# An encoder trunk in fp32: the gates' rows turned to one chunk per partition, the heads' rows repeated over the partitions by DMA, values projected first and the output gate last

## The chip, the core and the metric

The kernel runs on one core of a Trainium2 chip. The metric is the device time of one execution in microseconds (us). A core has a matrix engine (TensorE: PE in the profile, its weight loads PEld), a vector engine (VectorE: DVE), a scalar engine (ScalarE: ACT), a further elementwise engine (GpSimd: POOL) and a queue engine that here only issues transfers (SyncE: SP). Each engine works through its own instructions in order; semaphores hold an instruction until those of other engines, or transfers, are done. On chip, data lie in SBUF (128 partitions) and in PSUM, which the matrix engine writes. DRAM is the large memory off chip.

## What is computed

Two layers over a sequence of 1024 positions with width 1024. Each layer has an mLSTM group (4 heads of 128), a dilated attention group (8 heads of 64), an output projection and a feed-forward part of 4096. The change lies in the mLSTM group alone:

```
h = rms_norm(x, norm1_g); proj = h @ w_in
mq, mk, mv, mo, mi, mf, aq, ak, av = split(proj)
mq, mk = silu(depthwise_conv5([mq, mk]))
gi = mi + gate_i_b                       # 2 directions x 4 heads, a row of 1024 each
gf = log_sigmoid(mf + gate_f_b)
h_fwd = mlstm_chunkwise(q, k, v, gi[0], gf[0])
h_bwd = flip(mlstm_chunkwise(flip(q), flip(k), flip(v), flip(gi[1]), flip(gf[1])))
hm = headwise_rms(h_fwd + h_bwd) * head_norm_g
y_m = hm * sigmoid(mo)
```

Within a chunk the gates are needed as b = cumsum(lf), as a running maximum of li - b, and as a maximum m that is carried from chunk to chunk. Of these come a factor exp(li - b - max) for each pair of positions in a chunk, a factor for q against the state that comes in, and a decay of that state.

## The kernel before

Activations lie transposed: features on partitions, the 1024 positions in the free dimension. A projection (`proj`, 128 output features) is 48 matmuls 128x512: 8 blocks of input features, 2 halves of the positions (t = 0 and 1), and 3 products of split operands (`mm3`, lines 90 to 92). Its weights come in two loads of 256 KB on SP's queue (`wload`, line 73); each is split into a high part by ACT (line 80) and a low part by POOL (line 82), with three buffers for each of `wr`, `wh` and `wl`. The results stand in PSUM banks `pj` (three) and DVE copies them out, times the norm's factor r (`evac_r`, line 173).

`gates` makes one projection whose 128 rows repeat 16 gate rows (8 input, 8 forget), so every partition carries some gate row over all 1024 positions. All of the gates' arithmetic (lines 216 to 274) runs on 128x1024 tiles `g`: biases, log-sigmoid, two cumulative sums and two running maxima (`TENSOR_TENSOR_SCAN`, restarted at each chunk by a tile of resets), the chunk recurrence on tiles of 8 columns, and three exponentials. It leaves MT and inter (a row for each direction and head, repeated in each quarter of the partitions) and `nat`, in which three rows' worth of values are turned to one position per partition by 24 small transposes on PE (line 279) and three copies (line 280).

Then, for each head: `m_proj` projects the output gate (so, line 173), q and k (each with a 5-tap convolution, line 303, on DVE, and a sigmoid) and last v (zv), which PE transposes (line 327). `m_head` repeats the head's row of MT and of inter over all partitions with a stream shuffle on DVE, for both directions (E, line 340, and qi, line 347), adds the mask on POOL (341), subtracts on DVE (342) and takes the exponential on ACT (344). PE then turns k (358) and multiplies k with q (364), DVE multiplies E with that (366), and a chain over the 8 chunks in both directions follows, in which PE (378, 380, 389) and DVE (394) take turns for some 16 us. The matmuls of the next head's projections lie between those of the chain. `m_tail` normalises and gates the head's result; it was called between the next head's `m_proj` and its `m_head`.

The order on each engine is set by a scheduler that goes by the order of the code, by priorities (line 80 to 82 and 173 have a raised one) and by its own estimate of when each operand is ready. Tiles with a tag share a fixed number of buffers; a tile's first writer waits for the last reader of the tile that had the buffer. E, qi, kn and H of a head (and before them the gates' tiles) share the seven buffers of tag G.

## Time and profile before

| | us |
|---|---|
| median of 3 runs (2648.67 to 2659.3) | 2658.03 |
| the profiled execution, own time | 2652.92 |
| its span in the trace | 2651.2 |
| layer 0, norm's end and gates to the first chain over chunks | 24.9 to 110.3 |
| layer 0, to the second, third and fourth chain | 167.7, 233.3, 297.4 |
| layer 1, the same points | 1336.0, 1417.8, 1476.6, 1541.2, 1605.2 |

The profile is of one execution. Times within it count from the start of the span. A row of the timeline shows when an instruction began, its duration, engine, line, what it writes and reads, and in brackets how long the engine had been idle before it and what ended that. [...] Matmuls are pipelined, so two that follow one another overlap in the rows; what counts is the distance of their starts.

### The profile page before, as it was taken

Reading aid. Unit: us, or ns where it says so; the run is one execution under the profiler, and the core shown is the slowest. Engines: PE = TensorE matmul, PEld = TensorE weight load, DVE = VectorE, ACT = ScalarE, POOL = GpSimd, SP = SyncE. Lnnn points to the kernel's source line nnn. Section 1 sums busy time; section 2 is a strip of 40 time slices with the busy share of each in tenths; the row PEclk is TensorE's granted clock in tenths of the full one; section 3 lists DMA queues with packets and bytes.
Section 4 is the critical chain, followed back from the end, with each engine's and each line's share of the span. In section 5 each row is a group of like instructions: output and inputs, shape, how many; then the busy total and the mean of one; then the engine's idle time right before and its main releaser. Section 6 shows DMA issues by size and latency. Waiting matters only on the chain. (4 is left out here: it accounts for less than half of the span.)

```text
span 2651.2 us, 36031 instructions
## 1 busy us (share of the span) xinstructions
PE 2476.5 (93%) x13508; PEld 1958.3 (74%) x13508; DVE 1994.6 (75%) x2440; ACT 1269.2 (48%) x2092; POOL 1395.1 (53%) x1135
## 2 busy tenths in 40 slices
PE   7889989998999999999989898999988999999997
PEld 5777766665778888787767777666666788888876
DVE  7877656688887786968788776666788867869687
ACT  5433344464654545445534444444546445354554
POOL 5333332235677677767643333222256766677765
PEclk9999999998999999999999999999989999999998
DMA  4000110036455455555320011001355555456553
GB/s 134 29 27 30 36 35 21 25 108 148 96 111 112 103 108 112 110 109 111 85 75 29 32 33 35 24 25 38 107 132 96 112 113 107 107 104 115 112 104 84
DMA packets 113326, 214.07 MB, mean 81 GB/s; under 512 B 13424, under 2 KB 15616, under 8 KB 113152
## 3 DMA queue, kind: packets, MB, share of 16 engines
q0 software_dynamic: 46912, 93.06, 21.3%
q1 hardware_dynamic: 66240, 118.71, 14.6%
q8 instruction: 107, 1.75, 0.3%
q14 instruction: 67, 0.55, 0.1%
HBM read 203.33 MB, written 8.39 MB: 80 GB/s over the span
## 5 line engine op out<-in xcount | busy, mean ns | idle before, releaser
L82 POOL TENSOR_TENSOR wl<-w,wh 128x512 fp32r<-128x512 f32 x484 | 768.8, 1610 | 311.5 <-ACT wh L80 311.1
L812 PE MATMUL ph<-b,wh 128*128 128x512 f32 x2240 | 695.0, 392 | 13.6 <-DVE x L818 7.0
L812 PEld LDWEIGHTS ph<-b,wh 128*128 128x128 f32 x2240 | 422.6, 189 | 103.4 <-ACT wh L80 8.3
L80 ACT CAST wh<-w 128x512 fp32r<-128x512 f32 x484 | 298.2, 618 | 412.6 <-PE ph L812 119.3
L812 PE MATMUL ph<-b,wl 128*128 128x512 f32 x1120 | 441.5, 394 | 8.6 <-POOL wl L82 8.0
L82 POOL TENSOR_TENSOR wl<-wr,wh 128x512 fp32r<-128x512 f32 x132 | 198.6, 1506 | 470.6 <-ACT wh L80 385.4
L812 PE MATMUL pj<-b,wh 128*128 128x512 f32 x1224 | 383.6, 395 | 9.8 <-ACT wh L80 8.0
L90 PE MATMUL pj<-hh,wh 128*128 128x512 f32 x896 | 368.9, 412 | 18.0 <-DVE z L173 10.8
L92 PE MATMUL pj<-hh,wl 128*128 128x512 f32 x896 | 358.3, 400 | 1.2 <-POOL wl L82 0.6
L91 PE MATMUL pj<-hl,wh 128*128 128x512 f32 x896 | 358.5, 400 | 0.0
L761 DVE TENSOR_TENSOR b<-T,b 128x1024 fp32r<-128x1024 f32 x148 | 253.0, 1714 | 114.3 <-ACT b L760 110.9
L812 PEld LDWEIGHTS pj<-b,wh 128*128 128x128 f32 x1224 | 233.0, 191 | 61.2 <-ACT wh L80 9.8
L812 PEld LDWEIGHTS ph<-b,wl 128*128 128x128 f32 x1120 | 211.2, 189 | 64.8 <-POOL wl L82 21.5
L812 PE MATMUL pj<-b,wl 128*128 128x512 f32 x612 | 242.1, 396 | 8.9 <-POOL wl L82 8.9
L90 PEld LDWEIGHTS pj<-hh,wh 128*128 128x128 f32 x896 | 171.3, 191 | 68.8 <-issue 15.0
L92 PEld LDWEIGHTS pj<-hh,wl 128*128 128x128 f32 x896 | 171.1, 191 | 36.4 <-POOL wl L82 1.0
L91 PEld LDWEIGHTS pj<-hl,wh 128*128 128x128 f32 x896 | 171.4, 191 | 30.2 <-issue 0.5
L760 ACT CAST b<-T 128x1024 fp32r<-128x1024 f32 x148 | 155.6, 1051 | 58.0 <-DVE T L776 19.7
L600 ACT ACTIVATE sm<-sm,nm 128x512 f32<-128x512 f32 x128 | 91.6, 717 | 131.5 <-DVE nm L598 131.5
L788 POOL DMA_DIRECT2D w<-w_down x128 | 115.7, 933 | 73.6 <-DMA w<-w_down 23.2
L788 POOL DMA_DIRECT2D w<-w_up x128 | 113.0, 907 | 60.1 <-POOL wl L82 26.6
L812 PEld LDWEIGHTS pj<-b,wl 128*128 128x128 f32 x612 | 116.6, 191 | 36.7 <-POOL wl L82 12.4
(257 smaller groups left out, 4342.1 us busy)
## 6 DMA issues: line engine op xcount, KB each, us to landing
w<-w_up SPq DMA_DIRECT2D x128, 256.0 KB, 2.7
w<-w_up POOLq DMA_DIRECT2D x128, 256.0 KB, 4.2
w<-w_down SPq DMA_DIRECT2D x128, 256.0 KB, 2.7
w<-w_down POOLq DMA_DIRECT2D x128, 256.0 KB, 4.2
wr<-w_in SPq DMA_DIRECT2D x116, 256.0 KB, 2.7
w<-w_out SPq DMA_DIRECT2D x32, 256.0 KB, 5.2
w<-w_out POOLq DMA_DIRECT2D x32, 256.0 KB, 6.0
wr<-w_out SPq DMA_DIRECT2D x16, 256.0 KB, 2.8
```

The costliest lines, as they stand in the source:

```text
L80: nc.scalar.copy(wh, raw)
L82: nc.gpsimd.tensor_tensor(out=wl, in0=raw, in1=wh.bitcast(F32), op=ALU.subtract)
L90: nc.tensor.matmul(ps, wh[:, j, :], xh[:, sl], start=start, stop=False)
L91: nc.tensor.matmul(ps, wh[:, j, :], xl[:, sl], start=False, stop=False)
L92: nc.tensor.matmul(ps, wl[:, j, :], xh[:, sl], start=False, stop=stop)
L600: nc.scalar.activation(sm, sm, AF.Exp, scale=-1.0, bias=nm, accum_out=l)
L760: nc.scalar.copy(hi, src)
L761: nc.vector.tensor_tensor(out=lo, in0=src, in1=hi.bitcast(F32), op=ALU.subtract)
L788: self.nc.gpsimd.dma_start(w, src, accum_op=ALU.add)
L812: nc.tensor.matmul(out, a[:, k, :], b, start=new and k + i == 0, stop=k + i == 5, skip_group_check=not new)
```

## The change

`gates` now gives its work out in three steps (`next(gates, None)`, after the convolutions of q and of k in the first head's `m_proj`). The gate projection's rows, zt, are cut into their 8 chunks, and 8 small transfers on SP's queue bring them to one chunk and one gate row per partition (z: 16 rows x 8 chunks = 128 partitions, 128 positions each). All tiles of the gates' arithmetic are 128x128 from then on, in slices of two tiles X. What is carried between chunks lies across partitions now: a matmul with a 0/1 matrix `sel` (line 253, tile pa) collects it. MT and inter go to DRAM in 8 transfers (gd, line 269). The 24 small transposes become 3 of 128x128 (line 276) and one copy.

In `m_head` the shuffles of lines 340 and 347 are gone: E and qi are loaded by transfers that read the head's row of 4 KB in DRAM once for each partition (lines 339 and 346, 512 KB each, 4 for a head). `m_proj` projects v first (and turns it after q), then q, k, and the output gate last. `m_tail` of the head before is called inside `m_head`, behind the products of k and q.

```diff
     def gates(self, L, hs, acc, pl, order):
...
-        ws = [self.wload(self.a["w_in"][L, 1, :, 4 * i:4 * i + 4]) for i in range(2)]
+        ws = [self.wload(self.a["w_in"][L, 4, :, 4 * i:4 * i + 4]) for i in range(2)]
...
-        z = T()
+        zt = pl.tile([P, S + 2 * NC], F32, name="zt", tag="G", bufs=7)
         for t in range(2):
-            self.evac_r(z[:, t * HALF:(t + 1) * HALF], ps[t], r, t)
+            self.evac_r(zt[:, t * HALF:(t + 1) * HALF], ps[t], r, t)
+        room = [self.ya("X") for _ in range(2)]
+        rows = iter([x[:, i * P:(i + 1) * P] for x in room for i in range(NC)])
+        z, y, u, lf, lfa, lfF, lfB, bF, bB, b, e, MF, MB, w, fl, tiny = rows
+        for c in range(NC):
+            nc.sync.dma_start(z[16 * c:16 * c + 16], zt[0:16, c * P:(c + 1) * P])
...
+        yield r, nat
...
-        nc.vector.tensor_tensor_scan(out=bF, data0=rsF, data1=lfF, initial=0.0, op0=ALU.mult, op1=ALU.add)
+        nc.vector.tensor_tensor_scan(out=bF, data0=one, data1=lfF, initial=0.0, op0=ALU.mult, op1=ALU.add)
...
+        pa = self.mx.tile([P, 2 * NC], F32, name="pa", tag="t", bufs=1)
+        nc.tensor.matmul(pa, sel, at, start=True, stop=True)
+        nc.vector.tensor_copy(st, pa)
...
+        nc.scalar.activation(inter, MT, AF.Exp, scale=-1.0, bias=mps)
+        for c in range(NC):
+            nc.sync.dma_start(self.gd[L][:, :, c], out[16 * c:16 * c + 16])
...
+        yield
+        pt = self.mx.tile([P, 3, NC, 16], F32, name="pt", tag="s", bufs=2)
         for i, src in enumerate((e, w, fl)):
-            pt = self.mx.tile([P, NC, 32], F32, name="pt", tag="s", bufs=2)
-            for c in range(NC):
-                nc.tensor.transpose(pt[:, c], src[0:32, c * P:(c + 1) * P], self.ident[0:32, 0:32])
-            nc.vector.tensor_copy(nat[:, i], pt[:, :, 0:8])
-        return r, (MT, inter, nat)
+            nc.tensor.transpose(pt[:, i].rearrange("p c g -> p (c g)"), src, self.ident)
+        nc.vector.tensor_copy(nat, pt[:, :, :, 0:8])
+        yield
...
-            nc.vector.stream_shuffle(out=e.rearrange("p c t -> p (c t)"), in_=MT, mask=[row] * 32)
+            nc.sync.dma_start(e, bc(self.gd[L][row, 0].unsqueeze(0), [P, NC, P]))
...
-            nc.vector.stream_shuffle(out=x, in_=inter, mask=[row] * 32)
+            nc.sync.dma_start(x.rearrange("p (c t) -> p c t", t=P), bc(self.gd[L][row, 1].unsqueeze(0), [P, NC, P]))
...
+        if pend is not None:
+            self.m_tail(*pend)
```

On PE, in layer 0, the gates' first turned values (pt from g, line 279) stood inside the last matmuls of the first head's k projection (pj), before:

```order
L90 MATMUL pj<-hh,wh 128x512
L91 MATMUL pj<-hl,wh 128x512
L279 MATMUL pt<-ident,g_393 128x32 [waits DVE_49]
L279 MATMUL pt<-ident,g_393 128x32 x7
L92 MATMUL pj<-hh,wl 128x512
L90 MATMUL pj<-hh,wh 128x512 [waits Activation_49]
```

and now the one matmul that collects the chunks' values (pa) stands there, 30 matmuls into that projection:

```order
L91 MATMUL pj<-hl,wh 128x512
L92 MATMUL pj<-hh,wl 128x512
L253 MATMUL pa<-X,sel 128x16 [waits DMAHW4_49,DVE_49]
L90 MATMUL pj<-hh,wh 128x512
L91 MATMUL pj<-hl,wh 128x512
```

The turned values (line 276) follow behind the other 18 matmuls of the projection, so PE waits for the gates at two places, each in front of other matmuls. In layer 1 pa stands only 4 matmuls into the projection.

On SP, whose queue before held nothing but weight loads (wr) in this stretch, now, in layer 0, behind the eight gd transfers (line 269):

```order
L73 DMA wr<-w_in 128x512 [waits DMAHW7_49,Pool_49]
L339 DMA E<-gd_134 128x1024 [waits DMAHW4_49,DMAHW3_49,DMAHW5_49,DMAHW2_49,DMAHW6_49,DMAHW1_49,DMAHW0_49]
L346 DMA qi<-gd_134 128x1024
L339 DMA E<-gd_134 128x1024
L346 DMA qi<-gd_134 128x1024
L73 DMA wr<-w_in 128x512 [waits Pool_49] x2
L73 DMA wr<-w_in 128x512 [waits DMAHW7_49,Pool_49]
L339 DMA E<-gd_134 128x1024 [waits DVE_49,PE_49]
L73 DMA wr<-w_in 128x512 [waits DMAHW4_49,DMAHW0_49,Pool_49]
```

The first E waits for the eight gd transfers to land; the second head's E (with DVE_49 and PE_49) for the buffer that the first head's chain frees, and one weight load stands behind it.

On DVE, behind the first head's chain (C), the shuffle that makes the second head's E (lines 340, then 342) was DVE's own work, with copies of a projection (z, line 173) between, before:

```order
L340 STREAM_SHUFFLE E<-MT 128x1024 [waits PE_49]
L173 TENSOR_TENSOR z<-pj,r 128x512 [waits PE_49]
L394 SCALAR_TENSOR_TENSOR C<-C,dec,pk 128x129 [waits DVE_49]
L347 STREAM_SHUFFLE qi<-inter 128x1024
L394 SCALAR_TENSOR_TENSOR C<-C,dec,pk 128x129 [waits PE_49]
L405 SCALAR_TENSOR_TENSOR den<-H 128x8 [waits Activation_49]
L342 TENSOR_TENSOR E<-nat,E 128x1024 [waits Pool_49]
L173 TENSOR_TENSOR z<-pj,r 128x512 [waits PE_49]
```

and now both subtractions of E (line 341), which wait for the transfer and POOL's mask, stand ahead of the first copy of the second head's q projection:

```order
L341 TENSOR_TENSOR E<-nat,E 128x1024 [waits Pool_49]
L413 TENSOR_TENSOR H<-H 128x8x128 [waits Pool_49]
L348 COPY dec<-qi 128x8 [waits DMAHW1_49]
L417 TENSOR_REDUCE v_1202<-H 128x8 [waits Activation_49]
L341 TENSOR_TENSOR E<-nat,E 128x1024 [waits Pool_49]
L173 TENSOR_TENSOR z<-pj,r 128x512 [waits PE_49]
```

The shuffles are gone from DVE; what moved there is a wait for a transfer, with the copy of z behind it.

## Rows read from the trace of the kernel before

**Rows 1.** Page, part 1: busy us, share of span, instructions by engine.

```profile
PE 2476.5 (93%) x13508; PEld 1958.3 (74%) x13508; DVE 1994.6 (75%) x2440; ACT 1269.2 (48%) x2092; POOL 1395.1 (53%) x1135
```

**Rows 2.** Stretches: us, busy us (instructions) by engine, PE clock, DMA share, GB/s.

```profile
24.90:110.30 85.40, 72.35 (x321) 57.02 (x321) 73.79 (x81) 41.80 (x56) 38.05 (x30) 0.94 0.17 53
110.30:167.70 57.40, 50.81 (x273) 42.36 (x274) 43.89 (x63) 23.75 (x41) 20.07 (x15) 0.97 0.09 28
167.70:233.30 65.60, 58.52 (x314) 47.79 (x313) 49.06 (x66) 25.78 (x44) 24.73 (x17) 1.00 0.10 33
233.30:297.40 64.10, 60.19 (x323) 49.59 (x321) 47.61 (x67) 25.51 (x44) 22.57 (x12) 1.00 0.11 34
1336.00:1417.80 81.80, 69.21 (x319) 54.96 (x317) 67.68 (x72) 36.57 (x46) 35.34 (x27) 0.94 0.17 52
1417.80:1476.60 58.80, 53.01 (x268) 43.92 (x269) 43.51 (x62) 23.81 (x41) 19.00 (x15) 0.91 0.09 28
1476.60:1541.20 64.60, 58.04 (x313) 47.54 (x312) 49.03 (x65) 25.86 (x45) 24.06 (x17) 1.00 0.10 33
1541.20:1605.20 64.00, 60.02 (x322) 49.50 (x322) 47.52 (x65) 25.50 (x44) 22.61 (x12) 1.00 0.11 33
```

**Rows 3.** Timeline of PE: start us, us, instruction [idle before, releaser].

```profile
61.41 0.39 PE L90 MATMUL pj<-hh,wh 128*128 128x512 f32 x1
61.63 0.39 PE L91 MATMUL pj<-hl,wh 128*128 128x512 f32 x1
67.57 1.06 PE L279 MATMUL pt<-ident,g 32*128 32x32 f32 x8 [5.55 <-DVE g L236]
...
90.64 0.79 PE L90 MATMUL pj<-hh,wh 128*128 128x512 f32 x1 [4.27 <-DVE zv L173]
...
201.34 0.50 PE L90 MATMUL pj<-hh,wh 128*128 128x512 f32 x1 [2.97 <-DVE z L173]
...
1379.98 1.06 PE L279 MATMUL pt<-ident,g 32*128 32x32 f32 x8 [7.99 <-DVE g L236]
1398.61 0.50 PE L90 MATMUL pj<-hh,wh 128*128 128x512 f32 x1 [1.73 <-DVE zv L173]
```

**Rows 4.** PE's waits, 110 to 298 us: us in total, times, longest.

```profile
PE pj L90 <- DVE z L173: 6.4, 4, 3.0
PE pt L327 <- DVE zv L173: 5.9, 4, 4.5
```

**Rows 5.** Timeline of DVE in layer 0: gates, convolution, shuffle, one chain step.

```profile
43.11 0.69 DVE L173 TENSOR_TENSOR g<-ps,r 128x512 f32<-128x512 f32 x1
...
60.08 3.32 DVE L232 TENSOR_TENSOR_SCAN g<-rs,g 128x1024 f32<-128x1024 f32 x1
...
63.38 1.27 DVE L303 SCALAR_TENSOR_TENSOR c<-z,cw,c 128x1024 f32<-128x1024 f32 x1
...
96.49 1.31 DVE L340 STREAM_SHUFFLE E<-MT 128x1024 f32<-128x1024 f32 x1
...
113.99 0.35 DVE L394 SCALAR_TENSOR_TENSOR C<-C,dec,pk 128x129 f32<-128x129 f32 x1 [0.60 <-PE pk L389]
```

**Rows 6.** Timelines of ACT and POOL in layer 0: short instruction, E's mask.

```profile
97.88 2.41 POOL L341 TENSOR_TENSOR E<-E,cm 128x1024 f32<-128x1024 f32 x1 [0.75 <-DVE E L340]
...
108.28 0.39 ACT L387 ACTIVATE wv<-v,nat 128x129 f32<-128x129 f32 x1
```

**Rows 7.** DMA issues: queue, count, KB each, median us to landing; last row SP's issue (ns).

```profile
xd<-x POOLq DMA_DIRECT2D x8, 512.0 KB, 2.9
x<-xd POOLq DMA_DIRECT2D x8, 512.0 KB, 4.5
x<-x SPq DMA_DIRECT2D x7, 512.0 KB, 9.3
...
out<-x SPq DMA_DIRECT2D x16, 128.0 KB, 1.8
...
L73 SPq DMA_DIRECT2D wr<-w_in x116: 327/328/432, 1.2 to 1798.9; - x116
```

More of the change, by code (lines that the diff above doesn't have):

```diff
@@ L224, in gates @@
         nc.vector.tensor_tensor(out=lf, in0=lf, in1=u, op=ALU.add)
-        nc.vector.stream_shuffle(out=lfa, in_=lf, mask=[8 + i % 8 for i in range(32)])
-        mF, mB = self.dirm[:, 0:1], self.dirm[:, 1:2]
-        lfF, lfB = y, u
+        nc.vector.stream_shuffle(out=lfa, in_=lf, mask=[i // 16 * 16 + 8 + i % 8 for i in range(32)])
         nc.scalar.activation(lfF, lfa, AF.Copy, scale=mF)
         nc.scalar.activation(lfB, lfa, AF.Copy, scale=mB)
-        bF, bB, b = lf, lfa, T()
-        nc.vector.tensor_tensor_scan(out=bF, data0=rsF, data1=lfF, initial=0.0, op0=ALU.mult, op1=ALU.add)
@@ L232, in gates @@
-        nc.vector.tensor_tensor_scan(out=bB[:, ::-1], data0=rsB[:, ::-1], data1=lfB[:, ::-1], initial=0.0,
-                                     op0=ALU.mult, op1=ALU.add)
+        one = self.ones
+        nc.vector.tensor_tensor_scan(out=bF, data0=one, data1=lfF, initial=0.0, op0=ALU.mult, op1=ALU.add)
+        nc.vector.tensor_tensor_scan(out=bB[:, ::-1], data0=one, data1=lfB[:, ::-1], initial=0.0, op0=ALU.mult,
+                                     op1=ALU.add)
         nc.vector.tensor_tensor(out=b, in0=bF, in1=bB, op=ALU.add)
-        e = T()
@@ L236, in gates @@
         nc.vector.tensor_tensor(out=e, in0=z, in1=b, op=ALU.subtract)
[L237 to L241 removed]
+        nc.vector.tensor_tensor_scan(out=MF, data0=one, data1=e, initial=NEG, op0=ALU.mult, op1=ALU.max)
@@ new lines, in gates @@
+        nc.vector.tensor_scalar(out=v[:, 0:1], in0=MT[:, 0:1], scalar1=mB, scalar2=None, op0=ALU.mult)
+        nc.vector.scalar_tensor_tensor(out=v[:, 0:1], in0=MT[:, P - 1:P], scalar=mF, in1=v[:, 0:1], op0=ALU.mult,
+                                       op1=ALU.add)
+        nc.vector.tensor_tensor(out=v[:, 1:2], in0=bF[:, P - 1:P], in1=bB[:, 0:1], op=ALU.add)
+        for i in range(2):
+            nc.vector.tensor_scalar(out=at[:, NC * i:NC * i + NC], in0=chunk, scalar1=v[:, i:i + 1], scalar2=None,
+                                    op0=ALU.mult)
@@ L259, in gates @@
+        nc.vector.tensor_tensor_scan(out=mpB[:, 0:NC][:, ::-1], data0=ML[:, ::-1], data1=BL[:, ::-1], initial=NEG,
                                      op0=ALU.max, op1=ALU.add)
@@ L285, in m_proj @@
+        yield
+    def m_proj(self, L, h, hs, r, mp, gates):
         nc = self.nc
         base = 1 + 4 * h
-        so = mp.tile([P, S], F32, name="so", tag=f"so{h % 2}", bufs=1)
-        ps, self.ahead = self.ahead or self.proj(L, base, hs), None
+        ps, self.ahead = self.ahead or self.proj(L, base + 3, hs), None
+        zv = mp.tile([P, S + 4], F32, name="zv", tag="z", bufs=3)
         for t in range(2):
-            self.evac_r(so[:, t * HALF:(t + 1) * HALF], ps[t], r, t)
+            self.evac_r(zv[:, t * HALF:(t + 1) * HALF], ps[t], r, t)
+        v1 = mp.tile([P, NC, P + 1], F32, name="v1", tag=f"v1{h % 2}", bufs=1)
+        nc.gpsimd.memset(v1[:, :, P:P + 1], 1.0)
@@ L305, in m_proj @@
             qk.append(c)
+            next(gates, None)
+            if i == 0:
+                for g in range(2):
+                    pt = self.mx.tile([P, 4, P], F32, name="pt", tag="s", bufs=2)
+                    for c in range(4):
+                        nc.tensor.transpose(pt[:, c], zv[:, (4 * g + c) * P:(4 * g + c + 1) * P], self.ident)
+                    nc.scalar.copy(v1[:, 4 * g:4 * g + 4, 0:P], pt)
+        so = mp.tile([P, S], F32, name="so", tag=f"so{h % 2}", bufs=1)
+        ps = self.proj(L, base, hs)
+        for t in range(2):
+            self.evac_r(so[:, t * HALF:(t + 1) * HALF], ps[t], r, t)
         last = None
@@ L678, in layer @@
                                 ("v11", S + NC, 1), ("qk", S, 4), ("G", S + 2 * NC, 7)))
-                r, gt = self.gates(L, hs, acc, mp, order)
+                gates = self.gates(L, hs, acc, mp, order)
+                r, nat = next(gates)
                 pend = None
                 for h in range(MH):
-                    prj = self.m_proj(L, h, hs, r, mp)
-                    if pend is not None:
-                        self.m_tail(*pend)
+                    prj = self.m_proj(L, h, hs, r, mp, gates)
                     if h == MH - 1:
@@ L1096, in run @@
             self.xd = tc.dram_tile([P, KD, S], F32, name="xd")
+            self.gd = [tc.dram_tile([16, 2, NC, P], F32, name=f"gd{L}") for L in range(DEPTH)]
             for L in range(DEPTH):
```

83 lines of the change are left out of this document (26 added, 57 removed).

## The prediction

> **What bounds the kernel now.** I read the page's busy shares first: PE 93%, DVE 75% [rows 1]. PE is near its limit over the whole span, so the change can only win where PE stands idle, where its clock is down, or where PE work goes away. Hence the second view, the table of stretches, for the stage that the change touches [rows 2]. I cut it where each head's chain over the chunks begins. The idle time of PE is the stretch less its busy time. Layer 0: 85.40 - 72.35 = 13.1 us in the gates' stretch, then 6.6, 7.1 and 3.9. Layer 1: 12.6, then 5.8, 6.6 and 4.0. Of 541.7 us PE is idle in 59.6. In the gates' stretches DVE is 86% and 83% busy; there it is the bound. In a head's stretch DVE is 74 to 76% busy and PE 89 to 94%.
>
> Third, the timeline of PE [rows 3] names the long waits. 5.55 us for the gates' turned values (line 279) and 4.27 us for the copy of zv in layer 0; 7.99 and 1.73 in layer 1. The copy of zv was late because DVE was at work on the gates' 128x1024 tiles. In the heads, PE's waits are for copies out of PSUM (z 6.4 us in 4 waits, zv 5.9 in 4) [rows 4], on a DVE that also shuffles.
>
> Fourth, the clock. After the 4.27 us wait the next matmul took 0.79 us where 0.50 is the usual first one after a wait (so after the 2.97 us wait) [rows 3]. [...]
>
> **The change, part by part.**
>
> *The gates' arithmetic.* Tiles of 128x1024 become 128x128: the scan of 3.32 us, the convolution-sized passes of 1.27 us [rows 5] become instructions near the 0.35 us of DVE and the 0.39 us of ACT at 128x129 [rows 5, 6]. Some 16 DVE passes of 1.2 to 3.3 us go, about 22 us a layer; some 25 short ones of 0.2 to 0.4 us come, about 7. That is DVE time; the end moves only by what PE waits for. [...]
>
> *When the gates are ready, layer 0.* The last copy of the gate rows ends at 43.11 + 0.69 = 43.8 us [rows 5], as before. New behind it: four issues on SP at 0.33 us, and a landing. No transfer within SBUF is in the trace; from the nearest rows it lands 1.8 us (128 KB) to 2.9 us (512 KB, store) after issue [rows 7], so z is there at 46.9 to 48.0; I take 48.0. Up to pa, in DVE's and ACT's order: 6 short ACT instructions (2.4), 13 short DVE ones (4.6), two copies of z at 0.69 (1.4), the convolution's first ACT pass (1.2) and four DVE passes at 1.27 that stand between (5.1): 14.7 us, so pa can run at 62.7. PE gets there at: stop before at 67.57 - 5.55 = 62.0, less 16 matmuls at 0.22 (the distance of starts in [rows 3]: 61.63 - 61.41), plus 8 transposes of v that now stand ahead (0.17 each, 1.4) = 59.8. New wait: 2.9, and with a margin for hand-overs 3.4. Then 18 matmuls (4 us) cover the dozen short instructions up to the turned values (about 3.5 us): no second wait. In layer 1 pa stands 26 matmuls (5.9 us) earlier, but there no convolution passes stand ahead of it on DVE (6.3 us less), so I take 3.4 there too. So 5.55 + 4.27 and 7.99 + 1.73 go (19.5) and 6.8 comes.
>
> *The 24 small transposes* (8 in 1.06 us at the low clock [rows 3], so some 0.1 us each at the high one) become 3 and pa: 2 us a layer less on PE, 4 in all.
>
> *E and qi by transfer.* For the first head: results at about 65, 8 stores on SP (8 x 0.33 = 2.6), landing 2 more, then E: 512 KB. What this landing costs is the main unknown, as no transfer in the trace reads one row 128 times. Bounds from rows: 2.9 us (a store), 9.3 us (loads queued behind one another in the start) [rows 7]. I take the 4.5 us of the lone 512 KB loads from DRAM, the same size and direction. E is there at about 74; POOL's mask 2.41 [rows 6], DVE's subtraction 1.2 (a pass of the width of the 1.27): 77.6, and DVE's copy of so and product of k wait behind it. k is needed by PE when the so projection ends, about 78.6; the product comes at 79.6: 1 us of wait, plus 0.7 before the first chain step: 1.7 a layer, 3.4 in all. Of a landing up to 1 us later than taken, each us is added in full.
>
> [...]
>
> *Later heads.* Gone: four shuffles of 1.31 us [rows 5], 5.2 us of DVE a head. New: E cannot start before the chain of the head before frees its buffer (T), and DVE's copy of z stands behind both E. From T: E at 4.8 (issue and 4.5), mask 7.2, subtraction 8.5, POOL's share of the tail to 9.7, second mask 12.1, DVE's sum and reduction to 13.3, second subtraction 14.5, copy of z 15.2. PE needs that bank after the q projection (48 x 0.227 = 10.9), the transposes of v (1.4) and 12 matmuls (2.7): 15.0. So it is just late, and I take 1 us. At the head's end, k's convolution chain (ACT 1.2, four at 1.27, a sigmoid and a product of the same width at 1.1 and 1.2, and copies between) takes about the 10.9 us of the so projection that hides it: 0.5 us of wait; then q's product on POOL (2.7, a little over the mask's 2.41) holds the k x q matmuls 1 us and E times that 1.3, and 1.2 in the first chain steps where fewer projection matmuls stand between. Sum: 5 us a head, 3 heads, 2 layers: 30, against 17.6 + 16.3 = 33.9 us of idle time now. The weight load behind the second head's E belongs to a projection that begins over 20 us later; it is hidden, and would cost 1 us for each us beyond that.
>
> [...]
>
> **Sum:** gone 19.5 + 4 + 17.0 + 33.9 = 74.4; new 6.8 + 3.4 + 30 + 7 = 47.2; net 27 us. From the execution's own 2652.9 that is 2626 us. The median of the runs is 5 us above that execution and within its spread of 2648.7 to 2659.3; I make no correction but keep those 5 us in the range.
>
> **Rivals.**
>
> (a) *DVE's relief reaches PE further than I reckon.* For it: DVE's share of a head falls from 75% to some 67%, and every wait in [rows 4] is for DVE. If a head's waits come to 2.5 us instead of 5, and no clock falls remain: 15 + 7 better, 2604.
>
> (b) *Off the path.* PE is 93% busy and the heads' waits only change places; the transfers come at about 7 us instead of 4.5, which adds 2.5 us at each of 8 heads, 20 us: 2646. For it: under other traffic a 512 KB load took 9.3 us [rows 7]. Against it: the DMA share in this stage is 0.09 to 0.17 [rows 2].
>
> (c) *The repeated read is slow, and the kernel gets slower.* All 128 descriptors of a transfer read the same 4 KB; if these reads get in each other's way, DVE's in-order wait for E holds the copies of z and of so, and PE stops at each of the 8 heads, 1 us for each us of landing. The gain of 27 is gone at 4.5 + 27/8 = 7.9 us, and the kernel is slower by over 0.5% from 9.6 us; at 12 us: 2626 + 8 x 7.5 = 2686. For it: no row shows such a read. Against it: it is the same number of bytes as the loads that took 4.5.
>
> (d) *The turning in DRAM and SBUF does not come earlier.* If the small transfers take 6 us instead of 2 to 3, pa waits 3 us more in each layer: 2632, inside the range of the forecast.
>
> **How the numbers follow.** Forecast with (d) 0.50, (a) 0.20, (b) 0.17, (c) 0.13. Predicted: 2625 us. The range that leaves out no more than 2 in 10 goes from 2590 (a, with 15 us for what I could not see in the heads) to 2655 (b, with the spread of the runs and a landing near 8 us). A measurement of this kernel can tell about 0.5%, 13 us, from no change: faster means under 2645. The forecast and (a) are there, with half of (b) at its edge: faster 0.72; same 0.16; slower 0.12.
>
> **What would show it.** After, PE's timeline should have one wait at pa of some 3 us in place of the 5.55 and 7.99, no wait for zv, and a first chain at about 92 us in layer 0. The stretches between chains should be 60 to 64 us with PE idle for 4 to 6. E's transfer should land within 4 to 5 us. I am wrong if it lands at 8 or more, if DVE's waits for POOL at E take the place of the shuffles, or if the copy of z is late by over 3 us in each head.

## The result, and the profile after

The changed kernel takes 2632.25 us (median of 4 runs, 2630.3 to 2633.3); the kernel before takes 2654.86 us (median of 4, 2648.7 to 2659.3). The ratio is 0.9916 with a 95% interval of 0.9892 to 0.9940: faster by 0.8%, 22.6 us. The prediction was 2625, in a range of 2590 to 2655, with 0.72 for faster. The total was right; the way to it was not, as the rest of this text shows. Two executions of the kernel of run 11 below, of 3034 and 7415 us, are marked as slow in the record and left out.

The busy line of the page, which answers to [rows 1]:

```profile
PE 2466.7 (94%) x13470; PEld 1957.5 (74%) x13470; DVE 1923.8 (73%) x2376; ACT 1252.6 (48%) x2092; POOL 1405.3 (53%) x1119
```

DVE lost 71 us of busy time, PE 10. All of the edit lies between a layer's first gate matmul and the first copy of vt, where the attention begins. I call this the stage. It holds the same matmuls in every kernel here but for the small transposes, so its length and its PE busy time can be compared directly. The table of stretches for the stage in both layers (columns: stretch, its length, busy time and instructions of PE, PEld, DVE, ACT, POOL, clock granted to TensorE as a share of its full speed, DMA share, GB/s), of the kernel before:

```profile
6.90:338.20 331.30, 298.48 (x1498) 242.33 (x1499) 254.80 (x335) 141.74 (x227) 130.97 (x97) 0.98 0.15 49
1322.40:1647.00 324.60, 295.15 (x1498) 241.87 (x1499) 247.37 (x326) 132.45 (x217) 127.13 (x102) 0.96 0.13 40
```

and of the changed kernel:

```profile
6.80:324.20 317.40, 290.95 (x1476) 239.49 (x1477) 225.34 (x304) 134.20 (x227) 128.42 (x93) 0.98 0.24 78
1314.80:1627.80 313.00, 289.98 (x1476) 240.89 (x1477) 215.68 (x296) 124.95 (x217) 128.15 (x95) 0.97 0.22 69
```

The stage fell from 655.9 to 630.4 us, 25.5 us: 12.7 us of PE's busy time (298.48 + 295.15 against 290.95 + 289.98) and 12.8 us of its idle time. The rest of the program, where nothing was edited, took 1995 us in the profile before and 2000 us after; over all profiles of this study it lies between 1992 and 2009. That is the noise that a single total carries, so the experiments are read by the stage first and by the median second.

Inside the stage the gain is all in the later heads. Heads two to four, the stretches that answer to [rows 2]:

```profile
100.70:159.60 58.90, 53.21 (x284) 43.90 (x283) 42.99 (x54) 25.19 (x44) 22.24 (x12) 1.00 0.20 70
159.60:220.30 60.70, 59.16 (x320) 49.89 (x320) 43.74 (x59) 25.68 (x44) 24.73 (x17) 1.00 0.23 70
220.30:280.90 60.60, 59.18 (x320) 49.89 (x320) 43.61 (x58) 25.68 (x44) 25.43 (x16) 1.00 0.21 70
...
1404.30:1462.80 58.50, 53.11 (x283) 43.87 (x283) 42.57 (x54) 25.18 (x44) 22.05 (x12) 1.00 0.22 69
1462.80:1523.30 60.50, 59.12 (x320) 49.90 (x320) 43.57 (x58) 25.57 (x44) 25.63 (x17) 1.00 0.21 71
1523.30:1583.90 60.60, 59.17 (x320) 49.90 (x320) 43.62 (x58) 25.73 (x45) 25.46 (x16) 1.00 0.23 69
```

PE is idle there for 5.7, 1.5 and 1.4 us in layer 0 and 5.4, 1.4 and 1.4 in layer 1: 16.8 us in all, against 33.9 before, and the granted clock is 1.00 throughout. The first head is another matter. PE's timeline (start, duration, instruction, idle time before it and what ended that) has two long stops in each layer, where [rows 3] had the turned values:

```profile
64.29 0.61 PE L253 MATMUL pa<-X,sel 128*128 128x16 f32 x2 [6.56 <-DVE X L250]
88.80 1.94 PE L357 MATMUL pt<-ident,c 128*128 128x128 f32 x8 [6.43 <-DVE c L325]
...
1359.77 0.61 PE L253 MATMUL pa<-X,sel 128*128 128x16 f32 x2 [5.32 <-DVE X L250]
1392.07 1.94 PE L357 MATMUL pt<-ident,c 128*128 128x128 f32 x8 [7.59 <-DVE c L325]
```

25.9 us of waiting in place of the 19.5 that went. The second stop, the turning of k, is the one that the prediction had put at 1 us. DVE's timeline says why:

```profile
82.01 3.35 DVE L341 TENSOR_TENSOR E<-nat,E 128x1024 f32<-128x1024 f32 x1 [3.55 <-POOL E L340]
85.28 0.68 DVE L173 TENSOR_TENSOR so<-pj,r 128x512 f32<-128x512 f32 x1
85.88 2.77 DVE L325 TENSOR_TENSOR c<-c,sg 128x1024 f32<-128x1024 f32 x1
```

with POOL's beside it:

```profile
79.57 4.70 POOL L340 TENSOR_TENSOR E<-E,cm 128x1024 f32<-128x1024 f32 x2
84.24 3.33 POOL L325 TENSOR_TENSOR c<-c,sg 128x1024 f32<-128x1024 f32 x1
```

DVE stood for 3.55 us in front of E's subtraction, whose result PE's products need (after an exponential on ACT) only at 99.92, with k's product queued behind it, which PE was waiting for. And its instructions came out long: the subtraction takes 1.2 us elsewhere and 3.35 here, the product 1.22 elsewhere and 2.77 here. Each of the two ended about 1.1 us after POOL's instruction: the subtraction at 85.36, after the second mask at 84.27; the product at 88.65, after POOL's at 87.57. So a DVE instruction on 128x1024 that meets one of POOL's seems to stand until that one is done: it ends 1.1 us later, where alone it takes 1.2. The copy of so out of PSUM between them took its usual 0.68.

The transfers (per row: tiles, queue, count, KB each, median us from issue to landing):

```profile
E<-gd SPq DMA_DIRECT2D x16, 512.0 KB, 4.8
qi<-gd SPq DMA_DIRECT2D x16, 512.0 KB, 5.6
X<-zt SPq DMA_DIRECT2D x16, 8.0 KB, 2.7
gd<-out SPq DMA_DIRECT2D x16, 16.0 KB, 1.9
```

### The profile page after: what moved, and what is told of

It reads as the page before. It is cut to its first block, busy times and chain, and to the rows that moved or that the text cites. A ratio compares the mean times of both kernels' runs of the same rounds, so it can differ in the third digit from the quotient of the medians.

```text
span 2630.7 us, 35982 instructions
## 1 busy us (share of the span) xinstructions
PE 2466.7 (94%) x13470; PEld 1957.5 (74%) x13470; DVE 1923.8 (73%) x2376; ACT 1252.6 (48%) x2092; POOL 1405.3 (53%) x1119
## 5 line engine op out<-in xcount | busy, mean ns | idle before, releaser
L82 POOL TENSOR_TENSOR wl<-w,wh 128x512 fp32r<-128x512 f32 x484 | 782.7, 1636 | 303.8 <-ACT wh L80 303.3
L812 PE MATMUL pj<-b,wl 128*128 128x512 f32 x612 | 242.3, 396 | 13.5 <-POOL wl L82 13.5
L90 PEld LDWEIGHTS pj<-hh,wh 128*128 128x128 f32 x896 | 171.0, 191 | 54.7 <-issue 15.2
L80 ACT CAST wh<-wr 128x512 fp32r<-128x512 f32 x132 | 80.6, 614 | 139.4 <-PE pj L91 75.6
```

The costliest lines, as they stand in the source:

```text
L80: nc.scalar.copy(wh, raw)
L82: nc.gpsimd.tensor_tensor(out=wl, in0=raw, in1=wh.bitcast(F32), op=ALU.subtract)
L90: nc.tensor.matmul(ps, wh[:, j, :], xh[:, sl], start=start, stop=False)
L812: nc.tensor.matmul(out, a[:, k, :], b, start=new and k + i == 0, stop=k + i == 5, skip_group_check=not new)
```

## The experiments

Two questions. Which of the three parts (the order, the gates on 128x128, E and qi by transfer) brought the gain? And what holds the first head: the order on DVE, the landing of E, or POOL and DVE standing in each other's way?

**1. k's product ahead of E, first head only.** The masks and subtractions of E are held behind the products of the same engine.

```diff
-            nc.gpsimd.tensor_tensor(out=e, in0=e, in1=self.cm[:, d:d + 1].to_broadcast([P, NC, P]), op=ALU.add)
-            nc.vector.tensor_tensor(out=e, in0=nat[:, 0, :, row:row + 1].to_broadcast([P, NC, P]), in1=e,
-                                    op=ALU.subtract)
+            with self.after(h, 1):
+                nc.gpsimd.tensor_tensor(out=e, in0=e, in1=self.cm[:, d:d + 1].to_broadcast([P, NC, P]), op=ALU.add)
+            with self.after(h, 0):
+                nc.vector.tensor_tensor(out=e, in0=nat[:, 0, :, row:row + 1].to_broadcast([P, NC, P]), in1=e,
+                                        op=ALU.subtract)
...
+    def after(self, h, i):
+        return self.tc.issue_after(self.prod[i]) if h == 0 else nullcontext()
```

> The changed kernel with one difference: in the first head of a layer the subtraction of E on DVE is issued behind k's product with its sigmoid, and POOL's two masks of E behind q's product. Theory A (DVE's order makes the wait): in the changed kernel PE waits 6.4 us (layer 0) and 7.6 us (layer 1) for k's product at the turning of k, since DVE stands in front of it at E's subtraction, idle for 3.55 us until POOL's mask is done, then 3.35 us in a subtraction that takes 1.2 us elsewhere. With the product ahead the wait falls under 1.5 us in both layers, the first chain of layer 0 starts at 95 to 98 us instead of 102.3, and the kernel takes 2618 to 2623 us instead of 2632. Theory B (E itself is what is late): E is only made later, PE waits as long at the products of k and q with E or at the first chain step; the first chain stays within 2 us of 102.3 and the time within 4 us of 2632.

Measured: 2626.9 us (2625.7 to 2637.0), ratio 0.9902 [0.9881, 0.9922]; the stage 626.5 us, 3.9 less than the changed kernel. The first chain starts at 96.86, 5.5 us sooner, as theory A had it. PE's timeline:

```profile
84.45 1.06 PE L363 MATMUL pt<-ident,c 128*128 128x128 f32 x8 [2.12 <-DVE c L328]
95.20 0.71 PE L385 MATMUL pn<-v,E 128*128 128x129 f32 x4 [2.30 <-DVE E L371]
```

The wait at k fell from 6.4 and 7.6 us to 2.1 and 2.0: it was the order, though theory A had put the wait under 1.5 us and the time at 2618 to 2623. The two stretches of the stage, and the one behind the first chain in layer 0:

```profile
7.10:323.00 315.90, 294.15 (x1476) 242.03 (x1477) 225.10 (x304) 131.57 (x225) 127.35 (x93) 0.97 0.24 79
1313.70:1624.20 310.50, 292.48 (x1476) 243.03 (x1477) 218.87 (x296) 122.45 (x215) 125.48 (x95) 0.97 0.21 70
...
95.20:132.60 37.40, 34.53 (x188) 29.04 (x188) 24.47 (x39) 12.35 (x26) 11.95 (x12) 0.95 0.25 85
```

PE's idle time in the stage fell by 9.7 us, yet only 3.9 reached its end and some 5 the median: the same matmuls kept PE busy for 5.7 us more (586.6 against 580.9). The new waits (2.3 us for E, as above, 2.5 us at the products of k and q in layer 1, and 2.9 us for z in the second heads) add up to about as much as the second heads' other waits, which went; but the clock behind the first chain was 0.95, where the changed kernel had 1.00. At z, DVE was again held by POOL:

```profile
121.69 3.40 DVE L419 TENSOR_TENSOR H<-H 128x1024 f32<-128x1024 f32 x1 [2.02 <-POOL H L416]
...
131.88 1.28 DVE L176 TENSOR_TENSOR z<-pj,r 128x512 f32<-128x512 f32 x2
```

with POOL at its mask from 121.61 on:

```profile
121.61 2.40 POOL L345 TENSOR_TENSOR E<-E,cm 128x1024 f32<-128x1024 f32 x1
```

**2. The order alone, in the kernel before.** v first, the output gate last, the tail behind the products; the gates and the shuffles stay as they were.

```diff
-        ps, self.ahead = self.ahead or self.proj(L, base, hs), None
+        ps, self.ahead = self.ahead or self.proj(L, base + 3, hs), None
...
+        so = mp.tile([P, S], F32, name="so", tag=f"so{h % 2}", bufs=1)
+        ps = self.proj(L, base, hs)
...
-        ps = self.proj(L, base + 3, hs)
...
+        if pend is not None:
+            self.m_tail(*pend)
         H = [G("H", [P, NC, P + 2])[:, :, 0:P + 1] for d in range(2)]
```

> The kernel before with only the order changed: v projected first and turned after q, the output gate last, the tail of the head before behind the products of k and q. The gates' arithmetic, the 24 small transposes and the shuffles of E and qi stay as before. Theory A (the order carries the gain of the later heads): the stretches from chain to chain of heads 2 to 4 in layer 0 come to 59 to 61 us each, as in the changed kernel (58.5, 60.5, 60.6), with PE idle for 1 to 5 us in each; total 2628 to 2640 us, as the gates' part keeps its 13 us of idle time. Theory B (the shuffles' 5.2 us of DVE a head carry it): the stretches sum to 183 to 187 us, as before (57.6, 65.6, 64.0), and the time stays at 2645 to 2657 us.

Measured: 2645.2 us, ratio 0.9966 [0.9953, 0.9979]. The stage:

```profile
7.10:328.60 321.50, 295.23 (x1495) 243.17 (x1496) 252.67 (x334) 140.10 (x226) 127.70 (x101) 0.97 0.15 50
...
1317.90:1638.90 321.00, 292.91 (x1495) 241.80 (x1496) 246.63 (x327) 130.94 (x216) 125.14 (x102) 0.96 0.12 41
```

642.5 us: the order alone is worth 13.4 of the stage's 25.5. The stretches of heads two to four, counted from DVE's first chain step, come to 54.6, 58.3 and 62.5 us in layer 0, 175.4 in all against 187.2 before, and to 179.7 against 188.5 in layer 1, with the shuffles still on DVE; the changed kernel has 179.6 in either layer. So theory A holds for the heads: the order carries all that the later heads gained. The total lies at the edge of theory B's range, since the waits for the gates' turned values are still there (5.6 and 7.6 us), with a new one of 5.4 and 6.4 us for k's product in the second head, where the changed kernel waits 1.7.

**3. The changed kernel with E and qi by shuffle.** The gates' rows are read back once per layer into two tiles; the 32 transfers of 512 KB are gone.

```diff
-            nc.sync.dma_start(e, bc(self.gd[L][row, 0].unsqueeze(0), [P, NC, P]))
+            nc.vector.stream_shuffle(out=e.rearrange("p c t -> p (c t)"), in_=self.rowt[0], mask=[row] * 32)
...
-            nc.sync.dma_start(x.rearrange("p (c t) -> p c t", t=P), bc(self.gd[L][row, 1].unsqueeze(0), [P, NC, P]))
+            nc.vector.stream_shuffle(out=x, in_=self.rowt[1], mask=[row] * 32)
...
+        self.rowt = [self.ya(n) for n in ("MTr", "inr")]
+        for j in range(2):
+            for i in range(NC):
+                nc.sync.dma_start(self.rowt[j][16 * i:16 * i + 16].rearrange("p (c t) -> p c t", t=P), self.gd[L][:, j])
```

> The changed kernel, but E and qi are made by shuffles on DVE as before: the gates' rows are read back from DRAM once per layer (16 transfers of 64 KB into two tiles of 128x1024), and the 32 transfers of 512 KB are gone. Theory A (the order carries the gain of the later heads): the stretches of heads 2 to 4 stay at 59 to 62 us although DVE has 5.2 us more work in each; the time is within 8 us of 2632, the first head aside, whose E comes some 5 us later behind the 16 small transfers. Theory B (DVE's relief carries it): the stretches go back to 63 to 66 us with waits of PE for the copies z, 3 to 5 us for each of 6 heads, and the time is 2648 to 2662 us.

Measured: 2640.8 us (2634.0 to 2643.5), ratio 0.9942 [0.9921, 0.9964]; the stage:

```profile
7.10:332.30 325.20, 294.76 (x1476) 241.53 (x1477) 231.31 (x337) 131.35 (x225) 120.69 (x93) 0.96 0.17 54
...
1317.80:1629.40 311.60, 290.55 (x1476) 239.81 (x1477) 220.34 (x329) 122.36 (x215) 120.35 (x95) 0.97 0.14 46
```

636.8 us. The stretches of heads three and four are 60.7 and 62.5 in both layers, not 63 to 66: DVE's relief is worth little there, as theory A said. The steps of the stage are then 655.9, 642.5 (order), 636.8 (gates on 128x128), 630.4 (transfers): 13.4, 5.7 and 6.4 us. The medians give 10, 4 and 9, but the intervals of this kernel and of the order alone overlap, so the two smaller shares are rough. The gates' share is also a net one: here the first head's E comes behind the 16 transfers that read the rows back, and the first chain of layer 0 starts at 115.0 instead of 102.3.

**4. Every transfer of E and qi twice.**

```diff
             nc.sync.dma_start(e, bc(self.gd[L][row, 0].unsqueeze(0), [P, NC, P]))
+            nc.sync.dma_start(e, bc(self.gd[L][row, 0].unsqueeze(0), [P, NC, P]))
...
             nc.sync.dma_start(x.rearrange("p (c t) -> p c t", t=P), bc(self.gd[L][row, 1].unsqueeze(0), [P, NC, P]))
+            nc.sync.dma_start(x.rearrange("p (c t) -> p c t", t=P), bc(self.gd[L][row, 1].unsqueeze(0), [P, NC, P]))
```

> The changed kernel with every transfer of E and of qi made twice, one behind the other, into the same tile, so that E and qi are there some 5 us later. Prediction (each us of landing counts in full at all 8 heads): 8 x 4.8 = 38 us more, about 2670 us, with PE waiting for the copies z in the later heads. Rival A (the later heads have slack, only the first head of each layer is on the path): 2 x 5 to 10 us more, 2642 to 2652 us, and the stretches of heads 3 and 4 stay within 1 us of 60.6. Rival B (no transfer is on the path): within 5 us of 2632.

Measured: 2640.2 us, ratio 0.9939 [0.9925, 0.9954]; the stage 642.3 us, 11.9 more than the changed kernel. None of the three theories had this. The third and fourth stretch are 66.6 and 65.5 us in layer 0 and 64.6 and 65.3 in layer 1, against 60.5 to 60.6: 4 to 6 us each. But E came later than the 5 us that I had expected. POOL's mask of the second E in the third head, which starts when that has landed, in the changed kernel and here:

```profile
185.13 2.81 POOL L340 TENSOR_TENSOR E<-E,cm 128x1024 f32<-128x1024 f32 x1 [0.59 <-DMA E<-gd]
...
190.82 2.37 POOL L341 TENSOR_TENSOR E<-E,cm 128x1024 f32<-128x1024 f32 x1 [0.91 <-DMA E<-gd]
```

The chain of the head before began at 160.37 and at 156.01. Counted from there the second E is 10 us later, and 10 to 11 us later in the other three of these heads. Of the 4 to 6 us, 2.2 to 3.1 are PE's new wait for z and the rest is PE's own time: over the whole stage PE was busy for 591.7 us against 580.9, at a granted clock of 0.96 in both layers against 0.98 and 0.97. So landing does not count in full there: about half of it reaches the stretch. The first head got faster: its first chain starts at 96.80 instead of 102.32, with E there over 5 us later. DVE's timeline shows it:

```profile
81.53 1.22 DVE L325 TENSOR_TENSOR c<-c,sg 128x1024 f32<-128x1024 f32 x1
83.64 0.69 DVE L173 TENSOR_TENSOR so<-pj,r 128x512 f32<-128x512 f32 x1 [0.90 <-PE pj L92]
88.61 1.22 DVE L342 TENSOR_TENSOR E<-nat,E 128x1024 f32<-128x1024 f32 x1 [4.28 <-POOL E L341]
```

The scheduler that lists each engine's instructions put k's product in front of E, presumably as it took E to be late. PE does not wait at the turning of k in either layer. It is run 1 by another way, and shows the same: what held the first head was not E's landing but E's place. What PE waits for next is the products of k and q: 2.4 us in layer 0, and 5.4 in layer 1, where POOL still has E's mask in front of q's product.

**5. The order around the gates.** The convolution passes of q come behind the gates' last DVE instruction, and pa behind 36 matmuls of the k projection.

```diff
+        yield
         pa = self.mx.tile([P, 2 * NC], F32, name="pa", tag="t", bufs=1)
-        nc.tensor.matmul(pa, sel, at, start=True, stop=True)
+        with self.tc.issue_after(self.mms[11]), self.tc.high_priority(400):
+            nc.tensor.matmul(pa, sel, at, start=True, stop=True)
...
+            if h > 0:
+                conv(i)
+            elif i == 1:
+                next(gates)
+                with self.tc.issue_after(self.glast):
+                    conv(0)
+                conv(1)
             next(gates, None)
```

> The changed kernel with the first head's order around the gates changed: the convolution passes of q come behind the last of the gates' instructions on DVE instead of between them, and pa is put on PE behind 36 matmuls of the k projection (30 in layer 0 and 4 in layer 1 before). Theory A (the wait at pa is only slack in front of a later end: what sets the first chain is DVE's chain through E and k's product): pa's wait falls from 6.6 and 5.3 us to under 1, but the wait at the turning of k grows by as much; first chain in layer 0 within 2 us of 102.3, time 2628 to 2636 us. Theory B (the waits add up): the 12 us of both pa waits are won, 2618 to 2623 us.

Measured: 2620.1 us (2611.8 to 2622.4), ratio 0.9865 [0.9843, 0.9887]; the stage 617.3 us, 13.1 less than the changed kernel. Theory B came true. The wait at pa is gone, and the turning of k waits hardly longer than before (8.0 and 7.9 us, against 6.4 and 7.6), with the first chain at 97.16:

```profile
86.18 1.94 PE L372 MATMUL pt<-ident,c 128*128 128x128 f32 x8 [8.03 <-DVE dec L363]
```

The gain at pa was kept, but for 2 us: with four convolution passes out of their way the gates were ready sooner, so E was too, and k's product behind it. POOL's first mask and, behind both subtractions, k's product:

```profile
74.20 2.78 POOL L355 TENSOR_TENSOR E<-E,cm 128x1024 f32<-128x1024 f32 x1 [3.75 <-DMA E<-gd]
...
84.83 1.21 DVE L340 TENSOR_TENSOR c<-c,sg 128x1024 f32<-128x1024 f32 x1
```

**6. Runs 1 and 5 together.** The edits are those shown there.

> The changed kernel with both edits: gates ahead of q's convolution and pa later on PE, as in the run with these alone, and E's masks and subtractions behind the products of the first head. Theory A (with the order mended, PE's waits at pa go without coming back): pa under 1 us, the turning of k waits under 3 us, first chain in layer 0 at 91 to 94 us; 2614 to 2621 us. Theory B (DVE and POOL are the bound of the first head: instructions with two operands in SBUF never run on both at the same time in the trace, and between 60 and 97 us they add up to some 32 us): the wait only moves to the turning of k or to E, first chain not before 95.5 us, 2623 to 2630 us.

Measured: 2616.2 us, ratio 0.9861 [0.9846, 0.9875]; the stage 617.9 us, no shorter than run 5's. The time is in theory A's range, the first chain (96.18) in theory B's. PE waits 3.2 us at k and 2.8 us for E in layer 0, 0.9 and 6.7 in layer 1. DVE's and POOL's timelines between 80 and 91 us have one long instruction after the other (qi's product 3.37, two subtractions 5.64, POOL's two masks 6.72). With the order mended, the two engines were in each other's way.

**7. The mask of E on DVE instead of POOL, all heads.**

```diff
-            nc.gpsimd.tensor_tensor(out=e, in0=e, in1=self.cm[:, d:d + 1].to_broadcast([P, NC, P]), op=ALU.add)
+            nc.vector.tensor_tensor(out=e, in0=e, in1=self.cm[:, d:d + 1].to_broadcast([P, NC, P]), op=ALU.add)
```

> The changed kernel with the mask of E added on DVE instead of POOL in all heads; the order of the rest as the scheduler gives it. Theory A (the two engines exclude each other while both read SBUF: POOL's mask of 2.35 us takes as much from DVE as a DVE instruction, which does it in 1.2): E is ready sooner, the wait at the turning of k falls from 6.4 to 2 to 5 us, the long forms of DVE's subtraction of E (2.3 and 3.35 us) become 1.2, the stretches of heads 2 to 4 stay within 1 us; 2622 to 2631 us. Theory B (DVE is the scarce engine and POOL's help is real): 2.4 us more on DVE in each head makes the copies z late by 1 to 3 us, 2636 to 2650 us.

Measured: 2621.4 us (2621.0 to 2625.3), ratio 0.9883 [0.9869, 0.9898]; the stage 621.1 us, 9.3 less. The page's busy line:

```profile
PE 2467.6 (94%) x13470; PEld 1958.1 (75%) x13470; DVE 1931.9 (74%) x2392; ACT 1253.3 (48%) x2092; POOL 1352.1 (52%) x1103
```

Sixteen masks of at least 1.2 us were put on DVE, 19 us of work or more, and its busy time rose by 8 over the whole span; POOL lost 53. In the stage, where the masks are, DVE's busy time even fell, from 441.0 to 435.6 us, so the rest of its instructions there got more than 19 us shorter:

```profile
7.10:319.60 312.50, 292.16 (x1476) 240.80 (x1477) 221.82 (x313) 134.15 (x227) 104.11 (x85) 0.97 0.24 79
1309.10:1617.70 308.60, 290.13 (x1476) 241.27 (x1477) 213.78 (x304) 124.75 (x217) 105.61 (x87) 0.97 0.22 70
```

The subtraction of E by itself (min, median and max in ns, first start and last), of the changed kernel

```profile
L341 DVE TENSOR_TENSOR E<-nat,E x16: 1173/1843/3353, 82.0 to 1552.1; 128x1024 f32<-128x1024 f32 x16
```

and of this one

```profile
L341 DVE TENSOR_TENSOR E<-nat,E x16: 1207/1224/3282, 81.9 to 1539.9; 128x1024 f32<-128x1024 f32 x16
```

Theory A, if with a time 0.6 us below its range: POOL's help had cost as much as it gave. The wait at k fell to 3.9 and 4.5 us, and the later stretches stayed at 60.5 to 60.6.

**8. The mask on DVE and k's product first** (7 and 1; the masks behind k's product too).

> The changed kernel with the mask of E on DVE in all heads, and in the first head of a layer both masks and subtractions behind k's product. If the two effects are independent: the gain of the product's order (about 5 us) and that of the mask add, 2617 to 2626 us, with the wait at the turning of k under 2 us and none at the first chain's E. If DVE's load is what counts, the second head's copies of z wait longer than the 2.9 us that they wait with the product ahead alone, and the time is 2628 to 2640 us.

Measured: 2610.2 us, ratio 0.9838 [0.9821, 0.9856]; the stage 611.8 us. That is 18.6 us below the changed kernel's, where the two edits alone gave 3.9 and 9.3: they do more together than apart, and the time is below both forecasts. Of run 1's new waits, the one for E is 1.4 us in layer 0, and there is none for z; PE is busy for 578.2 us of the stage, against 586.6 in run 1.

**9. All three edits** (1, 5 and 7).

> The changed kernel with all three edits: gates ahead of q's convolution and pa later on PE, E's masks on DVE in all heads, and in the first head of a layer masks and subtractions of E behind k's product. If they are independent (the mask with the product first gave 2610, the order around the gates some 10 us more): pa's wait under 1 us, turning of k under 3.5 us, first chain of layer 0 at 90 to 92.5 us, 2598 to 2605 us. If DVE is the bound of the first head by now (eight convolution passes, two masks, two subtractions behind the gates), the 6 us at pa come back at the turning of k or at E: first chain not before 94 us, 2606 to 2613 us.

Measured: 2600.1 us (2594.1 to 2606.8), ratio 0.9796 [0.9762, 0.9830]; the stage 598.6 us, first chain at 91.89: as expected, they add.

**10. Run 8 with q's product on DVE too.**

```diff
-        for c, eng in zip(qk[::-1], (nc.vector, nc.gpsimd)):
+        for c, eng in zip(qk[::-1], (nc.vector, nc.vector)):
```

> The run with E's masks on DVE and k's product first, and the product of q with its sigmoid on DVE as well (POOL before, 2.4 to 3.4 us). If POOL's instruction shuts DVE out for its whole length: the product takes 1.2 us on DVE, the waits of 0.8 us for q's product go in all 8 heads and the first long mask after it (3.4 us) is 1.2; 2600 to 2607 us. If DVE's load counts: 1.2 us more in each head on DVE, waits for E before the chains grow, 2610 to 2618 us.

Measured: 2592.7 us (2586.8 to 2596.8), ratio 0.9766 [0.9733, 0.9798], 17.5 below run 8's, where I had expected 3 to 10. The stage is 598.3 us, 13.5 below run 8's:

```profile
6.40:309.80 303.40, 289.12 (x1470) 237.37 (x1471) 223.75 (x317) 132.63 (x230) 94.63 (x81) 0.99 0.25 81
1298.40:1593.30 294.90, 285.13 (x1470) 237.12 (x1471) 213.39 (x308) 123.20 (x220) 94.52 (x83) 0.98 0.23 73
```

In this kernel and the next the first copy of vt comes six matmuls earlier (1470, not 1476), which alone is about 1.4 us a layer; and the unedited rest of the program was some 8 us shorter in this profile than in run 8's. So the gain in the stage is 11 to 13.5 us. Eight products more on DVE are 10 us of work, and DVE's busy time in the stage is 437.1 us, against 437.5 in run 8 and 441.0 in the changed kernel.

The waits for E before the chains, 3.8 us in three heads of layer 1 in run 8, are no longer in the list of PE's waits.

**11. All of them** (9 and 10).

> All edits together: gates ahead of q's convolution, pa later, masks of E and the product of q on DVE, masks and subtractions of the first head behind k's product. If the gains add: 2590 to 2600 us. If DVE is the bound of the first head: within 4 us of the better of the two runs that have either the order around the gates or the product of q on DVE.

Measured: 2587.4 and 2592.6 us, two executions, so this kernel has no interval; the one lies in both forecast ranges and the other just under both. The stage is 594.1 us, 4.2 below run 10's, where the order around the gates had given 13.1 and 13.2 us in runs 5 and 9. By the stage, then, the gains do not add: most of that order's gain does not come on top of run 10's.

**12. Run 11 with the tail's second product on DVE.**

```diff
-            (nc.vector, nc.gpsimd)[d].tensor_tensor(out=H[d][:, :, 0:P], in0=H[d][:, :, 0:P],
+            nc.vector.tensor_tensor(out=H[d][:, :, 0:P], in0=H[d][:, :, 0:P],
```

> All edits of the run before (2587 to 2593 us in its undisturbed executions), and the tail's second product of H with the denominators on DVE too, so that POOL has only the splits of the weights left in a head. If POOL's help never pays there: DVE's waits for that product (2.1 us in four heads) go, time 2580 to 2590 us. If PE's waits in the later heads are gone already, so that the tail is off the path: no change, 2585 to 2594 us. If DVE becomes scarce: copies z late again, over 2595 us.

Measured: 2588.8 us (2587.9 to 2590.3), ratio 0.9755 [0.9739, 0.9770]; the stage is 587.8 us, 6.3 less than run 11's:

```profile
7.20:303.00 295.80, 286.77 (x1476) 236.97 (x1477) 227.79 (x320) 131.33 (x225) 80.93 (x77) 1.00 0.25 84
1293.70:1585.70 292.00, 285.49 (x1476) 238.31 (x1477) 220.82 (x313) 122.15 (x215) 80.42 (x79) 0.99 0.23 74
```

By the median it is what run 11 had: what the stage lost is within what the rest of the program varies, and the time lies in both of the first two ranges, so whether the tail is off the path stays open. The move was no longer free: DVE's busy time in the stage rose from 435.2 to 448.6 us, for some 10 us of work. This is the fastest kernel here with an interval: 2.5% below the kernel before, where the change itself gave 0.8%.

## Why the prediction was right, and where it was not

| term, both layers, us | predicted | measured |
|---|---|---|
| waits for the turned values and zv, gone | -19.5 | -19.5 |
| new wait at pa | +6.8 | +11.9 |
| first head, turning of k and first chain | +3.4 | +14.0 |
| later heads, idle 33.9 to | 30 (-3.9) | 16.8 (-17.1) |
| PE's own time (transposes, clock) | -14 | -12.7 |
| sum | -27 | -23.4 (stage: -25.5) |

The total came out because errors of 16 us one way (pa and the first head) and 13 us the other way (the later heads) nearly cancelled. That was luck, not the mechanism. The 2 us between the sum and the stage are in waits that the table does not list.

**The gates' wait** was mis-sized by 5.1 us. z was there when predicted (ACT's first instruction on it at 48.55, against 48.0), and each short instruction cost about what was reckoned: where I had 0.35 us, DVE's elementwise ones on 128x128 took 0.28 to 0.35 and its scans 0.39 to 0.43, but 1.10 and 1.16 where one met POOL. pa ran at 64.3 instead of 62.7: some of the instructions ahead of it met POOL's weight splits and took 1 us more (a convolution pass 2.29 instead of 1.28, a 128x1 instruction 1.25). And PE was there at 57.7, not 59.8.

**The first head** is the step that failed: "the product comes at 79.6: 1 us of wait". It came at 88.65, and PE waited 6.4 us, 7.6 in layer 1. Some 5 of the 9 us were E, whose mask began at 79.57, with E forecast for about 74: the eight stores to gd took SP 5.86 us to issue, where I had taken 2.6, and a weight load stood in front of E's transfer. The other 3.7 were put at nothing: the subtraction took 3.35 us and the product 2.77, both reckoned at 1.2. I had priced DVE's instructions as running beside POOL's next one, and they stood until that was done. Run 5 shows how far the list alone can hold it: there E's mask began at 74.20, as forecast, but both subtractions (2.30 and 3.35 us) stood in front of the product, and it came only at 86.0. Either part reached PE only because the product stood behind E, which I had seen and priced as if the chain in front were short: with the product ahead the wait is 2.1 and 2.0 us in run 1, and in run 4, where E lands over 5 us later still, there is none at the turning of k.

**The later heads** were better than forecast by 13 us. The reckoning of 5 us a head put 1.3 us there for E times the products, which is what the third and fourth heads lose (1.4 and 1.5 in all), and 3.7 for waits at z, at the products of k and q and at the first chain steps, which came in the second heads only. The relief of DVE by four shuffles a head was not what carried the gain: run 2 has it all with the shuffles in place. Nor did a us of landing cost a us: in run 4 some 10 us more cost 4 to 6 in the third and fourth heads. Rival (a) had named 2.5 us a head; it was 2.8, but by the order and not by DVE's relief, and the clock and the first head took the rest of its gain.

**The transfers** were sized about right: 4.8 us for E, 5.6 for qi, 4.5 taken. Rivals (b) and (c) needed 7 us and more, and run 4 shows that (c) would have hurt in the later heads, at about half the price that it named. E's 16 landings took 3.4 to 6.8 us each. The small transfers took 2.7 us and not 6, so (d) did not come about.

**The clock.** No run shows as a time the 17.0 us that the sum takes for the clock before, or the 7 that were to stay. What the traces show is the granted share: 1.00 or 0.50, with matmuls 128x512 starting 0.22 to 0.23 or 0.43 us apart. The loss, (1 - share) x length, is my estimate: 5.1 + 1.7 + 4.9 + 5.3 = 17.0 us over the gates' and the second heads' stretches before [rows 2], and 6.9 + 8.3 = 15.2 after, where the share was 0.91 over the gates' 76.8 us in layer 0, 0.89 over their 75.9 in layer 1 and 1.00 in the second heads. After the waits at pa and at k the granted clock was down for the next 6 to 8 us (columns as above):

```profile
64.30:72.00 7.70, 7.70 (x27) 6.23 (x28) 3.35 (x13) 1.73 (x5) 0.33 (x1) 0.69 0.06 13
...
88.80:95.00 6.20, 6.20 (x23) 5.32 (x24) 5.08 (x6) 3.40 (x3) 0.98 (x1) 0.66 0.12 42
...
1359.80:1368.00 8.20, 8.20 (x24) 6.61 (x25) 6.38 (x14) 0.63 (x2) 0.00 (x0) 0.61 0.12 34
1392.10:1399.00 6.90, 6.90 (x25) 5.83 (x26) 4.98 (x5) 3.40 (x3) 0.95 (x1) 0.65 0.11 38
```

By the same estimate this is 0.31 x 7.7 + 0.34 x 6.2 = 4.5 us in layer 0 and 5.6 us in layer 1, where half of the sum's 7 was 3.5; the other 5 of the 15.2 us lie in the waits themselves, where the share was 0.50 before PE went on. The falls of [rows 2] in the second heads (0.97 and 0.91) are gone.

What stays open: the shares of the gates on 128x128 and of the transfers, about 6 us each, rest on single profiles. Why the eight stores to gd take 0.73 us each to issue was not tried.

## What to carry to other kernels

An engine that runs its list in order can hold up a neighbour with an instruction that nobody needs yet (E's subtraction in front of k's product, for which PE waited 6.4 and 7.6 us); look in its list for what stands in front of the one that is waited for, before counting how late the transfer is. Work put on a second engine to relieve the first is only relief if the two can run at once: compare the duration of the same instruction alone and beside the other (E's subtraction: 1.2 and 3.35 us). Here, taking the masks and q's product back was worth about as much in the stage (9.3 and 11 to 13.5 us) as the change under study (25.5). And a total that comes out right is no proof of its terms: each needs its own line in the profile after.

## What the runs showed of the hardware

In the changed kernel's trace DVE's convolution passes (line 303, two operands in SBUF) and POOL's elementwise instructions did not run side by side: whichever began first kept its time, and the other stood until it was done. Of the 64 passes, 11 began during one of POOL's instructions. They took 2.19 to 2.29 us and ended 1.08 to 1.09 us after it, where the 40 that met none took 1.27 to 1.29. Thirteen others were under way when a weight split of POOL began; they kept their 1.29 us, and the split, 1.29 at the median, took 1.67 to 2.36. A small copy with its one operand in SBUF (dec, 128x8), 0.15 to 0.16 us alone, took up to 2.32 beside POOL. Not every instruction of DVE stood. Of the 64 copies of zv, z and so out of PSUM, 33 began during an instruction of POOL, and none of the 64 took over 0.69 us; and outside the stage reciprocals of 128x1 (line 602) began and ended within a weight split and took 0.14 to 0.16 us. What tells the two kinds apart was not tried. With the masks on DVE the median of E's subtraction fell from 1843 to 1224 ns, and 19 us of work moved to DVE did not make it busier in the stage (435.6 us, against 441.0).

A transfer that reads one 4 KB row of DRAM 128 times is not slow: 4.8 us at the median for 512 KB (3.4 to 6.8), where the loads of distinct data took 4.5 [rows 7].
